# Two passes behind each norm, queries scaled on ScalarE, 32-wide products issued in turn

## Chip, cores and metric

The kernel runs on one core of a Trainium2 chip. The metric is the device time of one execution in microseconds (us); lower is better. Before the change, three executions took 1079.45, 1079.23 and 1076.95 us (median 1079.23).

A core has five engines with instruction streams of their own. TensorE (PE) multiplies matrices; its weight loads are shown apart as PEld. VectorE (DVE) and ScalarE (ACT) do elementwise work, GpSimd (POOL) a little of it, and SyncE (SP) starts most transfers (DMA). Each engine works through its own stream in order and waits at semaphores for the others.

## What is computed

One block of a streaming encoder, on 512 tokens of width 1024, everything in float32: a half-step feed-forward network, a mixer, and a second half-step feed-forward network, each behind an RMS norm that is modulated by a condition vector `c`.

```python
def _modulate(x, shift, scale):
    return _rms(x) * (1.0 + scale[:, None, :]) + shift[:, None, :]
...
        h = _modulate(x, sh1, s1)
        x = x + 0.5 * g1[:, None, :] * _swiglu(h, ffn1_w_in[l], ffn1_w_out[l])
        h = _modulate(x, sh2, s2)
        y = _hybrid_mixer(h, cos, sin, w_in[l], gdn_conv_w[l], gdn_a_log[l], gdn_dt_bias[l],
...
        x = x + g2[:, None, :] * y
        h = _modulate(x, sh3, s3)
        x = x + 0.5 * g3[:, None, :] * _swiglu(h, ffn2_w_in[l], ffn2_w_out[l])
```

The mixer has two groups of four heads. One is a gated delta rule over chunks of 64 tokens, which needs, per chunk and head, the inverse of a unit lower triangular 64 x 64 matrix (`triangular_solve(M, rhs)` in the reference). The other is attention with low-rank queries and keys, whose queries and keys are RMS-normalised per head and carry a rotary part:

```python
    q_nope, q_rope = qf[..., :MLA_NOPE], qf[..., MLA_NOPE:]
...
    q_nope = _rms(q_nope, qkn_q_nope) * scale
    q_rope = _rope(_rms(q_rope, qkn_q_rope), cos[:, :, None], sin[:, :, None]) * scale
```

## The kernel before

Activations are held transposed: eight k-tiles of 128 channels by 512 tokens (`xT`, and the normalised `h`). A float32 product is made from three matmuls on rounded parts (`mm3`, L266 to L268): high weight by high activation, high weight by low activation, low weight by high activation. So each k-tile of `h` is a pair `hh`, `hl`, and each unit of weights (128 output columns by 1024) a pair `wh`, `wl`. `wr` is the raw weight that SP's queue has loaded; ACT casts it to `wh` (L193), and DVE subtracts for `wl` (L198). For a few units behind a norm (`dma=True`) ACT writes −`wr` into `wl` (L195) and a transfer on POOL's queue adds the rest (L196); this is the `wl<-wr` of the profile. PE writes results to the accumulators `pa` and `pb`.

**Stages**, by the time of the profiled execution: the condition vector's modulation and the first feed-forward network (to about 403 us), latents behind norm 2 (403 to 423), the dense units of the projections, with the delta rule's chain and attention beside them as generators that are advanced a step at a time (445 to 660), the recurrence and the output projection (660 to 715), norm 3 and the second feed-forward network (715 to 1076).

**Behind a norm** stands `first_units` (L489): `n` = 3 units at once, first for the first half of the tokens (256), then for the second. In the first half `lead` units go k-tile by k-tile, as `h` becomes ready, and the others follow whole. `nb` is the generator of the second half's norm (`norm_half`): its steps, taken at the places that `marks` lists, issue the column sum (`colsum`, L513, on PE), its scaling (`ve`, L519, on DVE), the spreading of the result (L441, on PE) and the modulation of the second half. Norm 2 uses `lead` 1 and marks (6, 15, 14), norm 3 `lead` 2 and marks (7, 18, 15). `modulate` makes `h`: DVE writes `hm` or `tm` (L459), ACT `hh` (L461), DVE `hl` (L453), the last one step behind. `matmuls_in_order` fixes PE's order in this part as the code is written. Elsewhere the tile scheduler orders each engine's instructions, so that an edit can move instructions far from it.

**`prep_q`** (from L1739) normalises the queries: squares on ACT, the reciprocal roots on DVE, then for the rotary part `qrx` (L1206) and `rope` (L1830 to L1834, into `qro`) on DVE, four transposes of `qro` on PE (L1768), and for the other part eight multiplications of `upo`, two heads each, on POOL (also L1206, the common helper `mul`). `head_tiles` then transposes `upo` on PE (L1725) and scales it on ACT into `nT`.

**`inverse`** builds the inverse by blocks, for four groups `p` of two chunks each: blocks of 16 and 32 by 128-wide products (L1553, L1559), then for `j` = 0 and 64 and four heads the products `T` by `at` (L1569) and `U` by `Y` (L1577), 32 x 32 each on a tile of PE's array given by `tile_position`, then 64-wide ones (L1587 to L1598). Between the groups' steps other work is interleaved by the scheduler: wide matmuls of the dense units and of `out_attended`, and the attention's `on`, transposed at L1900 once DVE has scaled it. In the dense units of the gate, ACT copies `pa` into `z` (L1921); the next unit needs the accumulator that this frees. ACT's table load stands ahead of the exponentials of the attention (`pr`, L168), whose bias `mx` DVE reduces (L1856).

Of the kernel before, what the change touches and what calls it, by code (L numbers as in the profile page):

```python
# [79 lines left out]
class Block:  # L80
# [408 lines left out]
    def first_units(self, n, nb, lead, marks):  # L489


        units = [self.next_unit(ahead=0) for _ in range(n)]
        ps = [self.acc() for _ in range(n)]
        first = [(kt, i) for kt in range(KT) for i in range(lead)] + [(kt, i) for i in range(lead, n) for kt in range(KT)]
        with self.matmuls_in_order(self.last_mm):
            for half in range(2):
                ts = slice(half * HALF, half * HALF + HALF)
                for at, (kt, i) in enumerate([(kt, i) for kt in range(KT) for i in range(n)] if half else first):
                    self.dense(ps[i], units[i], self.h, ts, kt, kt + 1)
                    if half == 0 and at in marks:  # L500
                        next(nb, None)
                if half == 0:
                    drain(nb)
                    self.prefetch(1)
        return ps
# [1027 lines left out]
    def inverse(self, p):  # L1533
# [32 lines left out]
        for j in (0, 64):  # L1566
            a, b = slice(j, j + 32), slice(j + 32, j + 64)
            for h in range(4):
                nc.tensor.matmul(py[b, 32 * h:32 * h + 32], at[a, h * P + j + 32:h * P + j + 64],  # L1569
                                 t[a, h * P + j:h * P + j + 32], start=True, stop=True, tile_position=(j, j + 32))  # L1570
            nc.scalar.copy(y[b, :P], py[b, :P])
        yield
        pz = self.aux()
        for j in (0, 64):
            a, b = slice(j, j + 32), slice(j + 32, j + 64)
            for h in range(4):
                nc.tensor.matmul(pz[a, 32 * h:32 * h + 32], y[b, 32 * h:32 * h + 32],  # L1577
                                 un[b, h * P + j + 32:h * P + j + 64], start=True, stop=True, tile_position=(j + 32, j))
            nc.vector.tensor_scalar(out=h4(un[a, :])[:, :, j + 32:j + 64],
# [150 lines left out]
    def prep_q(self, q):  # L1730
# [375 lines left out]
```

## Time and profile before

| | before |
|---|---|
| median of three executions | 1079.23 us (1076.95 to 1079.45) |
| profiled execution | 1077.71 us |
| its span, first to last instruction | 1076.0 us |
| mean granted TensorE clock | 0.987 of full speed |
| 128.63 MB read from memory, mean | 122 GB/s over the span |
| DMA, queue q1 | 41.1% of 16 engines' span |

The profile is of one execution. Each row of its lists names an engine, the line of the kernel, the operation and its tiles (output, arrow, inputs; buffer numbers are left out), and in a timeline the start in us from the beginning of the span and the length in us. What stands in square brackets is how long the engine stood idle before the row, and what released it. Matmuls overlap, so that their spacing tells more than their length. A matmul on float32 data is recorded as two, so a stretch of eight records is four matmuls of the program. The granted clock of TensorE is a number between 0 and 1 for a stretch of time; at 0.5 a matmul takes twice as long.

### The profile page before, as it was taken

Reading aid. Unit: us, or ns where it says so; the run is one execution under the profiler, and the core shown is the slowest. Engines: PE = TensorE matmul, PEld = TensorE weight load, DVE = VectorE, ACT = ScalarE, POOL = GpSimd, SP = SyncE. Lnnn points to the kernel's source line nnn. Section 1 sums busy time; section 2 is a strip of 40 time slices with the busy share of each in tenths; the row PEclk is TensorE's granted clock in tenths of the full one; section 3 lists DMA queues with packets and bytes.
Section 4 is the critical chain, followed back from the end, with each engine's and each line's share of the span. In section 5 each row is a group of like instructions: output and inputs, shape, how many; then the busy total and the mean of one; then the engine's idle time right before and its main releaser. Section 6 shows DMA issues by size and latency. Waiting matters only on the chain. (4 is left out here: it accounts for less than half of the span.)

```text
span 1076.0 us, 15659 instructions
## 1 busy us (share of the span) xinstructions
PE 1046.7 (97%) x6183; PEld 899.1 (84%) x6183; DVE 689.4 (64%) x1231; ACT 445.3 (41%) x761; POOL 51.3 (5%) x103
## 2 busy tenths in 40 slices
PE   6999999999999999998999899999999999999998
PEld 5788878788887898887778578988899999999997
DVE  4488983433577445558868644769768787777633
ACT  3342222222222245566575363465534444444322
POOL 1000000000000011102000030220000000000000
PEclk8999999999999999999999898999999999999999
DMA  9989963233698349411203001153432333233222
GB/s 274 277 240 310 301 203 99 81 98 93 199 289 263 95 120 240 113 49 40 79 25 92 26 21 39 40 126 91 129 107 79 118 115 98 83 118 99 67 71 79
DMA packets 203687, 136.85 MB, mean 127 GB/s; under 512 B 13777, under 2 KB 186590, under 8 KB 203614
## 3 DMA queue, kind: packets, MB, share of 16 engines
q1 hardware_dynamic: 202318, 131.14, 41.1%
q0 software_dynamic: 1296, 4.72, 2.4%
q8 instruction: 48, 0.79, 0.3%
q14 instruction: 25, 0.20, 0.1%
HBM read 128.63 MB, written 2.49 MB: 122 GB/s over the span
## 5 line engine op out<-in xcount | busy, mean ns | idle before, releaser
L266 PE MATMUL pa<-hh,wh 128*128 128x512 f32 (+1 forms) x597 | 227.0, 380 | 4.3 <-ACT z L1921 4.3
L268 PE MATMUL pa<-hh,wl 128*128 128x512 f32 (+1 forms) x597 | 225.0, 377 | 2.7 <-DMA wl<-wr 2.7
L267 PE MATMUL pa<-hl,wh 128*128 128x512 f32 (+1 forms) x597 | 224.8, 377 | 0.0
L193 ACT CAST wh<-wr 128x1024 fp32r<-128x1024 f32 (+1 forms) x106 | 108.0, 1019 | 258.3 <-PE pa L267 184.4
L198 DVE TENSOR_TENSOR wl<-wr,wh 128x1024 fp32r<-128x1024 f32 (+1 forms) x97 | 114.4, 1180 | 99.0 <-ACT wh L193 94.5
L266 PE MATMUL pa<-ah,wh 128*128 128x512 f32 (+1 forms) x396 | 145.5, 367 | 0.6 <-DVE xT L873 0.4
L267 PE MATMUL pa<-al,wh 128*128 128x512 f32 (+1 forms) x396 | 144.5, 365 | 0.0
L268 PE MATMUL pa<-ah,wl 128*128 128x512 f32 (+1 forms) x396 | 143.5, 362 | 0.0
L266 PEld LDWEIGHTS pa<-hh,wh 128*128 128x128 f32 x597 | 113.6, 190 | 27.2 <-ACT z L1921 4.7
L268 PEld LDWEIGHTS pa<-hh,wl 128*128 128x128 f32 x597 | 113.5, 190 | 23.1 <-DMA wl<-wr 3.3
L267 PEld LDWEIGHTS pa<-hl,wh 128*128 128x128 f32 x597 | 113.5, 190 | 19.2 <-DVE hl L453 0.4
L268 PEld LDWEIGHTS pa<-ah,wl 128*128 128x128 f32 x396 | 74.8, 189 | 12.0
L266 PEld LDWEIGHTS pa<-ah,wh 128*128 128x128 f32 x396 | 75.2, 190 | 10.4 <-ACT wh L193 1.7
L267 PEld LDWEIGHTS pa<-al,wh 128*128 128x128 f32 x396 | 75.2, 190 | 7.2
L551 DVE SCALAR_TENSOR_TENSOR aa<-ar,sc,aa 128x512 f32<-128x512 f32 x98 | 73.2, 751 | 9.7 <-DMA ar<-in_w_ada 8.5
L846 PE MATMUL pb<-fh,wh 128*128 128x256 f32 x144 | 40.7, 282 | 0.0
L848 PE MATMUL pb<-fh,wl 128*128 128x256 f32 x144 | 40.7, 283 | 0.0
L848 PE MATMUL pb<-hh,wl 128*128 128x256 f32 x144 | 40.7, 283 | 0.0
L847 PE MATMUL pb<-fl,wh 128*128 128x256 f32 x144 | 40.7, 282 | 0.0
L847 PE MATMUL pb<-hl,wh 128*128 128x256 f32 x144 | 40.7, 282 | 0.0
L846 PE MATMUL pb<-hh,wh 128*128 128x256 f32 x144 | 40.6, 282 | 0.0
L873 DVE SCALAR_TENSOR_TENSOR xT<-pa,mod,xT 128x512 f32<-128x512 f32 (+1 forms) x40 | 29.4, 736 | 17.5 <-PE pa L268 17.5
(433 smaller groups left out, 1995.0 us busy)
## 6 DMA issues: line engine op xcount, KB each, us to landing
wr<-in_ffn_w_in SPq DMA_DIRECT2D x82, 512.0 KB, 4.1
ar<-in_w_ada SPq DMA_DIRECT2D x48, 512.0 KB, 5.9
wr<-in_ffn_w_out SPq DMA_DIRECT2D x34, 512.0 KB, 3.4
ar<-in_w_ada SPq DMA_DIRECT2D x48, 256.0 KB, 4.8
wr<-in_w_in SPq DMA_DIRECT2D x21, 512.0 KB, 3.9
wr<-in_ffn_w_out SPq DMA_DIRECT2D x17, 384.0 KB, 3.4
wl<-wr POOLq DMA_DIRECT2D x9, 512.0 KB, 5.6
wr<-in_w_out SPq DMA_DIRECT2D x8, 512.0 KB, 4.8
```

The source lines that it names most:

```text
L193: self.nc.scalar.copy(hi, raw)
L198: self.nc.vector.tensor_tensor(out=lo, in0=raw, in1=hi.bitcast(F32), op=ALU.subtract)
L266: mm(out, wh, xh, start=start, stop=False)
L267: mm(out, wh, xl, start=False, stop=False)
L268: mm(out, wl, xh, start=False, stop=stop)
L551: nc.vector.scalar_tensor_tensor(out=acc, in0=a, scalar=sc, in1=acc, op0=ALU.mult, op1=ALU.add)
L846: mm(out, wh, xh, start=start and k == 0, stop=False, **kw)
L847: mm(out, wh, xl, start=False, stop=False, **kw)
L848: mm(out, wl, xh, start=False, stop=stop and k == 3, **kw)
L873: nc.vector.scalar_tensor_tensor(out=self.xT[t][:, ts], in0=p[:, ts], scalar=gate[:, t:t + 1], in1=self.xT[t][:, ts], op0=ALU.mult, op1=AL ...
```

## The change

Three edits, in `first_units`, `inverse` and `prep_q`.

```diff
@@ first_units
-                for at, (kt, i) in enumerate([(kt, i) for kt in range(KT) for i in range(n)] if half else first):
-                    self.dense(ps[i], units[i], self.h, ts, kt, kt + 1)
-                    if half == 0 and at in marks:
+                if half:
+                    for kt in range(KT):
+                        for i in range(n):
+                            self.dense(ps[i], units[i], self.h, ts, kt, kt + 1)
+                    continue
+                parts = [(kt, i, 0, x) for kt, i in first for x in range(2)]
+                parts += [(kt, i, 1, 0) for i in range(n) for kt in range(KT)]
+                for at, (kt, i, y, x) in enumerate(parts):
+                    nc.tensor.matmul(ps[i][:, ts], units[i][y][:, kt, :], self.h[kt][x][:, ts],
+                                     start=kt + x + y == 0, stop=y == 1 and kt == KT - 1)
+                    if at % 3 == 2 and at // 3 in marks:
                         next(nb, None)
-                if half == 0:
-                    drain(nb)
-                    self.prefetch(1)
+                drain(nb)
+                self.prefetch(1)
@@ inverse (and the same for pz, U and Y)
-        for j in (0, 64):
-            a, b = slice(j, j + 32), slice(j + 32, j + 64)
-            for h in range(4):
+        for h in range(4):
+            for j in (0, 64):
+                a, b = slice(j, j + 32), slice(j + 32, j + 64)
                 nc.tensor.matmul(py[b, 32 * h:32 * h + 32], at[a, h * P + j + 32:h * P + j + 64],
                                  t[a, h * P + j:h * P + j + 32], start=True, stop=True, tile_position=(j, j + 32))
+        for j in (0, 64):
+            b = slice(j + 32, j + 64)
             nc.scalar.copy(y[b, :P], py[b, :P])
@@ prep_q
-                qv = q[b][g][:, :384].rearrange("p (h d) -> p h d", h=2)[:, :, :128]
-                self.mul(qv, qv, self.bc(rqn[:, 4 * b + 2 * g:4 * b + 2 * g + 2], 2), nc.gpsimd)
+                for e in range(2):
+                    qv, c = q[b][g][:, 192 * e:192 * e + P], 4 * b + 2 * g + e
+                    nc.scalar.activation(qv, qv, AF.Copy, scale=rqn[:, c:c + 1])
```

In the first half of the tokens, `first_units` issues all products with the high weights first (`hh` and `hl` of each k-tile), unit by unit as before, and all products with the low weights behind them. The same matmuls are issued in another order, and the norm's steps are counted by every third matmul. In `inverse`, the products for `j` = 0 and `j` = 64 alternate, and the two copies of their results follow both. In `prep_q`, sixteen activations on ACT, one for each head and block of tokens, do what eight multiplications on POOL did.

**PE in norm 3.** The program's PE stream at the start of norm 3; `pa_6522` and `pa_6523` are the accumulators of the two leading units (`pa_6530` and `pa_6531` after the change), with weights `wh`, `wl` of their own. Before:

```order
3044 L266 MATMUL pa_6522<-hh_6301,wh_6368 128x256
3045 L267 MATMUL pa_6522<-hl_6302,wh_6368 128x256
3046 L268 MATMUL pa_6522<-hh_6301,wl_6369 128x256
3047 L266 MATMUL pa_6523<-hh_6301,wh_6419 128x256
3048 L267 MATMUL pa_6523<-hl_6302,wh_6419 128x256
3049 L268 MATMUL pa_6523<-hh_6301,wl_6420 128x256
3050 L266 MATMUL pa_6522<-hh_6303,wh_6368 128x256
```

After:

```order
3034 L507 MATMUL pa_6530<-hh_6309,wh_6376 128x256
3035 L507 MATMUL pa_6530<-hl_6310,wh_6376 128x256
3036 L507 MATMUL pa_6531<-hh_6309,wh_6427 128x256
3037 L507 MATMUL pa_6531<-hl_6310,wh_6427 128x256
3038 L507 MATMUL pa_6530<-hh_6311,wh_6376 128x256
...
3082 L507 MATMUL pa_6532<-hl_6324,wh_6474 128x256
3083 L441 MATMUL pb_6591<-dg_6564,ones_97 128x256
3084 L507 MATMUL pa_6530<-hh_6309,wl_6377 128x256
```

Four matmuls of each k-tile of `h` stand where six stood, and the first product with a low weight now stands behind all 48 with high ones and behind the spreading at L441. The column sum keeps its place, behind six k-tiles of the two leading units. On DVE, the `tm` of the last k-tile moves ahead of `ve`.

**ACT in `prep_q`.** ACT's stream where the attention's queries are scaled; `cv` is a convolution's result, `l2q` and `ktk` come from transposed keys of the delta rule, `wh` is the next unit's high weight. Before:

```order
259 L1320 ACTIVATE vn_4041<-pa_4205,ry_3787 128x256
260 L168 ACTIVATE cv_4200<-cv_4200 128x512
261 L1430 ACTIVATE l2q_4269<-pb_4264 128x512
262 L1433 COPY ktk_4271<-pb_4264 128x512
263 L193 CAST wh_4625<-wr_4624 128x1024
```

After:

```order
260 L1789 ACTIVATE upo_3832<-upo_3832,sq_4094 128x128 x2
261 L1789 ACTIVATE upo_3916<-upo_3916,sq_4094 128x128
262 L168 ACTIVATE cv_4200<-cv_4200 128x512
263 L1789 ACTIVATE upo_3916<-upo_3916,sq_4094 128x128
264 L1789 ACTIVATE upo_3850<-upo_3850,sq_4094 128x128 x2
265 L1789 ACTIVATE upo_3934<-upo_3934,sq_4094 128x128 x2
266 L1438 ACTIVATE l2q_4269<-pb_4264 128x512
267 L1441 COPY ktk_4271<-pb_4264 128x512
268 L1789 ACTIVATE upo_3868<-upo_3868,sq_4094 128x128 x2
269 L1789 ACTIVATE upo_3952<-upo_3952,sq_4094 128x128 x2
270 L1789 ACTIVATE upo_3886<-upo_3886,sq_4094 128x128 x2
271 L1789 ACTIVATE upo_3970<-upo_3970,sq_4094 128x128 x2
```

Eight activations stand ahead of `l2q` and eight between `ktk` and the cast of `wh`, which follows next. The eight multiplications leave POOL's stream; nothing takes their place there.

**PE beside the attention.** PE's stream where a dense unit of the gate ends, with the transposes of `on` and the scores `nT` by `nT`. Before:

```order
2601 L266 MATMUL pa_5349<-hh_3169,wh_5227 128x512
2602 L1900 MATMUL pb_5182<-ident_92,on_5180 128x128 x4
2603 L1553 MATMUL pb_5197<-t_5193,at_4551 128x128 x4
2604 L1847 MATMUL pb_5204<-nT_4530,nT_4359 128x256
2605 L1847 MATMUL pb_5205<-nT_4543,nT_4384 128x256
2606 L1850 MATMUL pb_5204<-krT_4426,qrT_4298 128x256
2607 L1850 MATMUL pb_5205<-krT_4426,qrT_4298 128x256
2608 L267 MATMUL pa_5349<-hl_3170,wh_5227 128x512
2609 L268 MATMUL pa_5349<-hh_3169,wl_5228 128x512
```

After:

```order
2601 L266 MATMUL pa_5357<-hh_3169,wh_5235 128x512
2602 L267 MATMUL pa_5357<-hl_3170,wh_5235 128x512
2603 L268 MATMUL pa_5357<-hh_3169,wl_5236 128x512
2604 L1913 MATMUL pb_5190<-ident_92,on_5188 128x128 x4
2605 L1561 MATMUL pb_5205<-t_5201,at_4559 128x128 x4
2606 L1860 MATMUL pb_5212<-nT_4538,nT_4367 128x256
```

The unit's last two matmuls moved ahead of the transposes of `on`. Further on in the same stream stand the small products of the four groups, `U` by `Y`. Before (`pb_5572` is group 0, `pb_5590` 1, `pb_5601` 2, `pb_5622` 3):

```order
2700 L1577 MATMUL pb_5572<-U_5331,Y_5441 32x32 x4
2701 L1577 MATMUL pb_5590<-U_5361,Y_5479 32x32 x4
2702 L1577 MATMUL pb_5601<-U_5397,Y_5513 32x32 x4
2703 L1577 MATMUL pb_5572<-U_5331,Y_5441 32x32 x4
2704 L1577 MATMUL pb_5622<-U_5423,Y_5544 32x32 x2
...
2712 L267 MATMUL pa_5618<-ml_5563,wh_5466 128x512
2713 L1577 MATMUL pb_5601<-U_5397,Y_5513 32x32 x4
2714 L1587 MATMUL pb_5650<-ident_92,U_5397 64x64
2715 L1577 MATMUL pb_5622<-U_5423,Y_5544 32x32 x4
```

After:

```order
2696 L1587 MATMUL pb_5580<-U_5339,Y_5449 32x32 x8
2697 L1587 MATMUL pb_5598<-U_5369,Y_5487 32x32 x8
2698 L1587 MATMUL pb_5609<-U_5405,Y_5521 32x32 x8
2699 L1587 MATMUL pb_5630<-U_5431,Y_5552 32x32 x8
2700 L1599 MATMUL pb_5641<-ident_92,U_5339 64x64 x4
2701 L266 MATMUL pa_5626<-mh_5570,wh_5474 128x512
```

Each group's eight products now stand together, `j` = 0 and 64 in turn, and the four groups one behind the other; before, three stretches held them. For `T` by `at`, seven stretches become three in the same way. The transposes of `U` (L1587 before, L1599 after), three pieces before, are four after, with wide matmuls between them.

More of the change, by code (lines that the diff above doesn't have):

```diff
@@ L489, in first_units @@
     def first_units(self, n, nb, lead, marks):
+        nc = self.nc
         units = [self.next_unit(ahead=0) for _ in range(n)]
@@ L1573, in inverse @@
         pz = self.aux()
-        for j in (0, 64):
-            a, b = slice(j, j + 32), slice(j + 32, j + 64)
-            for h in range(4):
+        for h in range(4):
+            for j in (0, 64):
+                a, b = slice(j, j + 32), slice(j + 32, j + 64)
                 nc.tensor.matmul(pz[a, 32 * h:32 * h + 32], y[b, 32 * h:32 * h + 32],
                                  un[b, h * P + j + 32:h * P + j + 64], start=True, stop=True, tile_position=(j + 32, j))
+        for j in (0, 64):
+            a = slice(j, j + 32)
             nc.vector.tensor_scalar(out=h4(un[a, :])[:, :, j + 32:j + 64],
```

## The prediction

> **What bounds the kernel now.** I read first the busy table of the page, then PE's waits over the whole span (columns: total us, times, longest us), then windows around the stages that the change touches (columns: busy us of PE, PEld, DVE, ACT and POOL, then the granted clock, DMA share and GB/s).
>
> ```profile
> PE 1046.7 (97%) x6183; PEld 899.1 (84%) x6183; DVE 689.4 (64%) x1231; ACT 445.3 (41%) x761; POOL 51.3 (5%) x103
> ```
> ```profile
> PE pa L266 <- ACT z L1921: 4.3, 1, 4.3
> PE pb L1768 <- DVE qro L1834: 2.8, 2, 2.6
> PE pa L268 <- DMA wl<-wr: 2.7, 2, 2.0
> PE pb L1900 <- DVE on L1206: 1.8, 3, 0.9
> ```
> ```profile
> 598.60:605.50 6.90, 4.89 (x17) 4.22 (x18) 3.89 (x6) 2.55 (x7) 0.00 (x0) 0.51 0.25 76
> 642.00:654.00 12.00, 12.00 (x82) 10.24 (x83) 4.68 (x8) 2.92 (x7) 0.00 (x0) 0.57 0.03 7
> 718.10:721.50 3.40, 3.40 (x16) 3.40 (x17) 2.35 (x6) 1.88 (x5) 0.84 (x1) 0.50 1.09 249
> ```
>
> TensorE is busy for 97% of 1076.0 us. The change removes no matmul, so it can only win idle time of PE (1076.0 − 1046.7 = 29 us, much of it at the start), matmul time spent at half clock (the three windows), and time between small products. Four waits are in its reach, 11.6 us together.
>
> **The queries on ScalarE.** Rows of PE, POOL, DVE and ACT around the start of `prep_q`'s products, then the durations of DVE's operations over the whole run (min/median/max in ns), then ACT's operations on 128x128 (mean ns of one behind the busy time).
>
> ```profile
> 497.02 0.66 PE L1768 MATMUL pb<-ident,qro 128*128 128x128 f32 x4 [2.60 <-DVE qro L1834]
> 490.80 5.62 POOL L1206 TENSOR_TENSOR upo<-upo,sq 128x256 f32<-128x256 f32 x8 [23.95 <-DVE sq L189]
> 491.25 2.17 DVE L1206 TENSOR_TENSOR qrx<-upo,sq 128x128 f32<-128x128 f32 x4
> 493.45 0.99 DVE L1830 TENSOR_TENSOR rt<-qrx,rope 128x512 f32<-128x512 f32 x1
> 494.36 1.58 DVE L1833 TENSOR_TENSOR rt<-qrx,rope 128x256 f32<-128x256 f32 x2
> L1206 DVE TENSOR_TENSOR qrx<-upo,sq x8: 277/295/699, 491.2 to 498.1; 128x128 f32<-128x128 f32 x8
> L1833 DVE TENSOR_TENSOR rt<-qrx,rope x4: 417/623/829, 494.4 to 499.3; 128x256 f32<-128x256 f32 x4
> L1830 DVE TENSOR_TENSOR rt<-qrx,rope x2: 691/840/989, 493.5 to 498.4; 128x512 f32<-128x512 f32 x2
> 499.28 1.05 ACT L193 CAST wh<-wr 128x1024 fp32r<-128x1024 f32 x1 [5.59 <-PE pa L267]
> L1879 ACT COPY ao<-pb 128x128 f32<-128x128 f32 x16 | 4.1, 266 | 6.3 <-PE pb L1877 6.1
> L1660 ACT ACTIVATE o<-pb,eG 128x128 f32<-128x128 f32 x12 | 3.4, 370 | 4.7 <-PE pb L1658 4.7
> ```
>
> PE waits 2.60 us for `qro`, which DVE makes while POOL multiplies (490.80 to 496.42). Each kind of DVE operation has its longest duration there and its shortest after POOL is done: 0.70 against 0.28 us, 0.83 against 0.42, 0.99 against 0.69. Without POOL's eight rows the four `qrx` take about 4 × 0.28 instead of 2.17 (−1.05), L1830 −0.30, the two L1833 −0.74 and L1834, of L1830's shape, −0.30: together −2.4, and up to −2.6 with the gaps between them. `qro` is then there at 494.4 to 494.6, and PE arrives at 497.02 − 2.60 = 494.42. ACT takes 16 activations for this, 16 × 0.27 to 16 × 0.37 = 4.3 to 5.9 us by the two rows. The order puts eight ahead of `l2q` and eight between `ktk` and the `wh` cast, into a gap of 5.59 us in which ACT waits for PE to free `wh`. With PE 2.6 earlier that gap is some 3 us, but half of the activations run ahead of it, in ACT's earlier idle time. At 0.27 us ACT is done at about 496.6, when the cast may start (499.28 − 2.6); at 0.37 the cast is 1.5 late. Bounds: −2.6 and 0 (nothing won if as much is waited for ACT); I take **−2.5**, because the wait's own row shows what DVE loses.
>
> **The stall before `z`.** The order moves, by the scheduler, the last two matmuls of a dense unit (L267, L268) ahead of the transposes of `on`, of the inverse's 128-wide products and of the scores.
>
> ```profile
> 595.59 0.50 PE L267 MATMUL pa<-hl,wh 128*128 128x512 f32 x1
> 600.61 0.80 PE L266 MATMUL pa<-hh,wh 128*128 128x512 f32 x1 [4.29 <-ACT z L1921]
> 596.12 1.05 ACT L193 CAST wh<-wr 128x1024 fp32r<-128x1024 f32 x1 [6.80 <-PE pa L267]
> 597.19 1.28 ACT L168 ACT_TABLE_LOAD   x1
> 595.88 0.42 DVE L1856 TENSOR_REDUCE mx<-pb 128x1 f32<-128x256 f32 x1
> ```
>
> Before, the cast waits for that L267, and the table load, the exponentials and the copy `z` queue behind it on ACT. Moved up, L267 is done some 3 us sooner, and the cast with it. The table load then waits for `mx` only, 595.88 + 0.42 = 596.30 instead of 597.19: **−0.9**. Bounds: 0 (if something else holds the cast) and −2.6, if the first 1.7 us of the half clock behind the stall go too; I keep the half clock, since 3.4 us of waiting remain.
>
> **The products of 32 in the block inverse.** PE's rows at one stretch, and at the long one.
>
> ```profile
> 633.17 0.39 PE L267 MATMUL pa<-ml,wh 128*128 128x512 f32 x1
> 633.40 0.40 PE L268 MATMUL pa<-mh,wl 128*128 128x512 f32 x1
> 633.73 0.43 PE L1569 MATMUL pb<-T,at 32*32 32x32 f32 x8
> 634.09 0.50 PE L267 MATMUL pa<-ml,wh 128*128 128x512 f32 x1
> 634.43 0.39 PE L268 MATMUL pa<-mh,wl 128*128 128x512 f32 x1
> 637.13 1.52 PE L1577 MATMUL pb<-U,Y 32*32 32x32 f32 x48
> ```
>
> The 48 records at 637.13 take 1.52 us, some 30 ns each, so the 64 of each kind take 1.9 us. One stretch of 8 costs more than its products: from 633.40 to 634.43 stand two wide matmuls (0.23 each, as from 633.17 to 633.40) and 8 × 0.03, 0.70 in all; 1.03 pass, so a stretch costs 0.33 beside its products. In the order the stretches of `T,at` go from seven to three and those of `U,Y` from three to one, while the 64-wide transposes of `U` stand in one piece more. Taken alone that is 1.3 less for `T,at`, but PE waits there for `on` (1.8 us in three waits, the last row of that table above), and what comes earlier mostly lengthens those: I count −0.3 (bounds 0 and −1.3). For `U,Y` and after it, nothing waits like that: 0.33 × (2 − 1) = −0.3, and what neighbours on different tiles save by overlapping, which no row isolates; it lies between 0 and half of 1.9, and I take −0.7. The clock is 0.57 over the 12 us behind this (642 to 654), about 12 × 0.43 = 5 us lost; moving the small products may take or add one window of 3.4 us (1.7 us either way), which I count at 0. Sum **−1.3**, bounds +1.7 and −4. [...]
>
> **First token half, norm 3 (FFN2).** PE's and DVE's rows.
>
> ```profile
> 718.01 0.51 PE L268 MATMUL pa<-hh,wl 128*128 128x256 f32 x1 [1.96 <-DMA wl<-wr]
> 725.21 0.59 PE L441 MATMUL pb<-dg,ones 128*128 128x256 f32 x2
> 719.36 0.88 DVE L453 SCALAR_TENSOR_TENSOR hl<-tm,mod,hh 128x256 fp32r<-128x256 f32 x2
> 722.42 0.16 DVE L519 TENSOR_SCALAR ve<-pb 128x2 f32<-128x2 f32 x1 [1.80 <-PE pb L513]
> 723.56 0.49 DVE L453 SCALAR_TENSOR_TENSOR hl<-tm,mod,hh 128x256 fp32r<-128x256 f32 x1 [0.18 <-ACT hh L461]
> ```
>
> The wait of 1.96 us for a low weight goes, and with it a window at half clock: by the third window above its 16 matmuls take 3.40/16 = 0.21 us at clock 0.50, so some 0.12 at full clock (the half and a little), and 1.5 us are lost. That looks like −3.5. But the high pass uses a k-tile's four matmuls in 0.48 us, where the six of before took 0.72, and `h` isn't ready so early: `hl` of k-tiles 4 and 5 ends at 720.24. So PE now waits for DVE: k-tile 5 ends at 720.24 + 0.5, colsum at 721.1. `ve` (now behind `tm` of k-tile 7) follows at 721.3 instead of 722.42, `hl` of k-tile 7 ends near 722.3 instead of 724.05, and k-tile 7 is through at 722.8. With 16 high matmuls of the third unit (1.92) L441 starts at 724.7 against 725.21, and 24 matmuls follow in both: −0.5. If these waits leave a window at half clock, about 24 matmuls cost 0.09 more: +1.6. I take **0**, between them and nearer the first; the full −3.5 is the lower end of this term.
>
> **Norm 2 (latents).** Here no low weight is waited for, PE waits for `na` alone, and the next row is the last `hl`.
>
> ```profile
> 407.21 0.58 PE L513 MATMUL pb<-ones,na 128*128 128x1 f32 x4 [1.27 <-DVE na L477]
> 406.25 0.48 DVE L453 SCALAR_TENSOR_TENSOR hl<-hm,mod,hh 128x256 fp32r<-128x256 f32 x1 [0.86 <-ACT hh L461]
> ```
>
> The one leading unit now has two matmuls for a k-tile instead of three and meets `hl` of k-tile 7 at 406.73; by the marks five more matmuls (0.6) and then colsum follow, at about 407.5: **+0.3**; with a window at half clock +1.9.
>
> When does a window at half clock follow? Three more windows, each 3.4 us ahead of the time in question:
>
> ```profile
> 714.70:718.10 3.40, 1.44 (x13) 1.23 (x11) 2.69 (x7) 3.40 (x6) 0.85 (x1) 1.00 0.98 165
> 595.20:598.60 3.40, 1.12 (x6) 0.35 (x4) 2.30 (x5) 2.45 (x3) 0.00 (x0) 1.00 0.00 0
> 404.05:407.45 3.40, 2.13 (x17) 1.75 (x15) 1.53 (x4) 2.47 (x5) 1.66 (x3) 1.00 0.99 183
> ```
>
> The first two, with PE busy for 42% and 33%, were followed by half clock; the third, with 63% (norm 2 as it is), was not. What I work out for the changed norms lies between the last two kinds (about 1.9 of 3.4 us at both, 56%), nearer the third, which is why the forecast keeps full clock and the other outcome stays in. [...]
>
> **Sum**: −2.5 − 0.9 − 1.3 + 0 + 0.3 = −4.4 us. The remaining reordering (`kro`, attention from 545 to 563) I count at nothing, because the wide matmuls there are the same and only fill other waits. Against the profiled execution (1077.7 us: span 1076.0 and 1.7 around it) this gives 1073.3; that execution lies 1.5 below the median of the runs (1079.2), so I put the time between, at **1074.0** (0.7 above the sum, as with the rivals). A measurement of this kernel can tell about 0.3% (3.2 us) from no change.
>
> **Rivals.**
> - The first half is bound by `h`, not weights, and both norms get a window at half clock: +1.9 and +1.6 instead of +0.3 and 0, so −1.2 in all, 1077.2. For it: the 42% window. Chance 0.25, with the case in which ACT's activations give back half of the 2.5.
> - Everything goes: norm 3 wins its 3.5, and the inverse is rid of a half-clock window: −4.4 − 3.5 − 1.7 = −9.6, 1068.8. Against it: DVE's rows of `hl`. Chance 0.1.
> - The small products don't overlap and the removed stretches end in the wait for `on`: −4.4 + 1.3 = −3.1, 1075.3; the change doesn't do there what it says. Chance 0.1.
> - Slower: ScalarE becomes the bound in `prep_q`. If one activation with a scale from memory takes d, the cast is 16 × d − 4.4 us late; above d = 0.43 (2.5 us late) this part's gain is gone, above 0.55 the whole sum, and at 0.75 it is 7.6 late: +3.2, 1081.6. Against it: the 0.27 and 0.37 rows. Chance 0.08.
> - Forecast: 0.47.
>
> The forecast's own spread (about ±2) puts a quarter of its chance (0.12) within 0.3%, with all of the first rival and half of the third: faster 0.35 + 0.1 + 0.05 = 0.50, within 0.42, slower 0.08. The range goes from the second rival to beyond the first, 1068.5 to 1079.0, and leaves out the slower case and the edges.
>
> **What would show it.** Right: no POOL rows in `prep_q`, 16 activations of about 0.3 us, and the wait for `qro` under 0.3; the wait for `z` near 3.4; in norm 3 no wait for `wl<-wr` but three or four short ones for `hl`, with L441 at most 0.5 earlier than now; `U,Y` in one stretch of about 1.2 us. Wrong: clock 0.5 around either norm, the `wh` cast behind the activations as PE's releaser, or a wait for `on` that grows by more than the stretches give.

## The result and the profile after

The changed kernel takes **1074.13 us** (median of 21 executions, 1071.31 to 1079.33) against 1078.64 us of the kernel before (21 executions): ratio **0.9959**, 95% interval 0.9947 to 0.997, so 3 to 6 us or 0.4% faster. The profiled execution took 1074.32 us, span 1072.6, mean granted clock 0.989.

First PE's waits in the changed kernel, as before (total us, times, longest):

```profile
PE pa L266 <- ACT z L1934: 4.1, 1, 4.1
PE pb L1913 <- DVE on L1214: 3.2, 3, 1.6
PE pa L507 <- ACT hh L461: 1.6, 3, 0.8
PE pa L268 <- DMA wl<-wr: 0.9, 1, 0.9
PE pa L507 <- DVE hl L453: 0.7, 2, 0.5
```

The wait for `qro` (2.6 us) is gone and that for `wl` at norm 3 too (the 0.9 is a later one, 0.72 before). In their place stand 2.3 us for `hh` and `hl` at the norms, and the wait for `on` grew from 1.8 to 3.2. The waits of the four rows that I had in reach add up to 8.2 us instead of 11.6, plus those 2.3 new ones.

Windows of the changed kernel (busy us of PE, PEld, DVE, ACT, POOL; then the clock):

```profile
404.20:407.60 3.40, 2.40 (x13) 1.60 (x13) 1.40 (x4) 2.34 (x5) 1.68 (x3) 1.00 1.07 221
407.60:411.00 3.40, 3.40 (x18) 3.40 (x17) 0.64 (x3) 0.00 (x0) 0.82 (x2) 0.50 1.10 225
598.70:605.60 6.90, 6.00 (x22) 5.21 (x23) 4.06 (x6) 1.43 (x3) 0.00 (x0) 0.51 0.00 0
642.00:654.00 12.00, 12.00 (x108) 10.46 (x107) 6.39 (x11) 3.81 (x7) 0.00 (x0) 1.00 0.15 45
714.80:721.60 6.80, 6.58 (x32) 6.28 (x31) 2.01 (x7) 0.91 (x2) 0.88 (x1) 0.50 1.02 237
```

In this pair of profiles half clock is new at norm 2 (407.6 to 411.0), twice as long at norm 3 (6.8 us against 3.4), the same behind `z`, and gone behind the inverse: 642 to 654 had clock 0.57 before and has 1.00 now. It is one execution of each kernel; the profiles of the experiments show further down which of this belongs to the change.

**Where the time went.** The same instruction's start in both profiled executions, and how the lead changes:

| PE's instruction | before | after | lead | change on the way |
|---|---|---|---|---|
| first matmul behind norm 2 | 403.00 | 403.05 | +0.05 | |
| L441 behind norm 2 | 410.60 | 412.46 | +1.86 | +1.8, another +0.2 at a later `wl` |
| first transpose of `qro` | 497.02 | 496.34 | −0.68 | −2.7 |
| first matmul behind the wait for `z` | 600.61 | 599.60 | −1.01 | −0.3 |
| first of `U,Y`, 32 wide | 637.13 | 636.29 | −0.84 | +0.2 |
| first matmul behind norm 3 | 715.29 | 709.67 | −5.62 | −4.8 |
| L441 behind norm 3 | 725.21 | 721.86 | −3.35 | +2.3 |

From there to the end nothing changes (the spans differ by 3.4). So in this pair the norms cost 4.3, the queries won 2.7, and the stretch behind the first `U,Y` won 4.8, nearly all of it by the clock: 10.2 us at half clock are 5.1 lost.

**A measure for the clock.** Every execution reports its span and its mean granted clock. While PE is busy, time at half clock is about half lost: there 512-wide matmuls follow one another every 0.427 us against 0.227 at full clock, and 128-wide ones on float32 data every 0.213 against 0.109 (both profiles). So (1 − clock) × span is about what half clock cost that execution, and the time less this is what it would take at full clock. For the 21 executions of the changed kernel the first is 11.3 us in the mean and the second 1063.0 with a standard deviation of 0.6, while the times themselves spread over 8 us. The spread is the clock's. Both numbers stand with each experiment below; before has 13.5 to 15.7 and 1063.8 to 1064.4 in its 83 executions beside them. By these means the change is worth about 1 us at full clock (0.8 to 1.4), and the larger part of its gain is half clock (2.2 to 4.4).

### The profile page after: what moved, and what is told of

It reads as the page before. It is cut to its first block, busy times and chain, and to the rows that moved or that the text cites. A ratio compares the mean times of both kernels' runs of the same rounds, so it can differ in the third digit from the quotient of the medians.

```text
span 1072.6 us, 15669 instructions
## 1 busy us (share of the span) xinstructions
PE 1044.5 (97%) x6183; PEld 897.1 (84%) x6183; DVE 687.2 (64%) x1231; ACT 448.2 (42%) x777; POOL 45.6 (4%) x95
## 4 chain that ended last, share of the span: by engine, by line
PE 86%; DVE 5%; ACT 5%; DMA 2%; issue 1%; POOL 1%; SPq 0%; POOLq 0%; DVEq 0%; ACTq 0%
PE pa L266 19%; PE pa L267 19%; PE pa L268 19%; PE pb L854 5%; PE pb L855 5%; PE pb L856 5%; PE pa L507 2%; PE pb L1860 1%; PE pb L414 1%; PE pb L266 1%; PE pb L267 1%; PE pb L268 1%; PE pb L1476 1%; PE pb L1863 1%; DVE wl L198 1%
## 5 line engine op out<-in xcount | busy, mean ns | idle before, releaser
L266 PE MATMUL pa<-hh,wh 128*128 128x512 f32 (+1 forms) x549 | 212.6, 387 | 4.1 <-ACT z L1934 4.1
L268 PE MATMUL pa<-hh,wl 128*128 128x512 f32 (+1 forms) x549 | 210.2, 383 | 0.9 <-DMA wl<-wr 0.9
L267 PE MATMUL pa<-hl,wh 128*128 128x512 f32 (+1 forms) x549 | 210.3, 383 | 0.0
L267 PE MATMUL pa<-al,wh 128*128 128x512 f32 (+1 forms) x396 | 144.5, 365 | 0.0
L266 PEld LDWEIGHTS pa<-hh,wh 128*128 128x128 f32 x549 | 103.6, 189 | 27.0 <-ACT z L1934 4.5
L268 PEld LDWEIGHTS pa<-hh,wl 128*128 128x128 f32 x549 | 103.6, 189 | 21.2 <-DMA wl<-wr 1.4
L267 PEld LDWEIGHTS pa<-hl,wh 128*128 128x128 f32 x549 | 103.7, 189 | 18.6 <-issue 0.3
L267 PEld LDWEIGHTS pa<-al,wh 128*128 128x128 f32 x396 | 75.2, 190 | 7.2
L559 DVE SCALAR_TENSOR_TENSOR aa<-ar,sc,aa 128x512 f32<-128x512 f32 x98 | 73.1, 750 | 12.5 <-DMA ar<-in_w_ada 11.3
```

What stands on the lines that cost most here:

```text
L266: mm(out, wh, xh, start=start, stop=False)
L267: mm(out, wh, xl, start=False, stop=False)
L268: mm(out, wl, xh, start=False, stop=stop)
L559: nc.vector.scalar_tensor_tensor(out=acc, in0=a, scalar=sc, in1=acc, op0=ALU.mult, op1=ALU.add)
```

## Experiments

The kernel before ran beside them each time, on the same chip. In all tables "lost" is (1 − clock) × span and "rest" the time less that, means in us.

### The three parts apart

`x1_queries` has the hunk of `prep_q` alone, `x2_inverse` the two of `inverse`, `x3_first` that of `first_units`; `x4_no_first` is the changed kernel without the last:

```diff
 x4_no_first, in the changed kernel
-                parts = [(kt, i, 0, x) for kt, i in first for x in range(2)]
-                parts += [(kt, i, 1, 0) for i in range(n) for kt in range(KT)]
...
+                for at, (kt, i) in enumerate([(kt, i) for kt in range(KT) for i in range(n)] if half else first):
+                    self.dense(ps[i], units[i], self.h, ts, kt, kt + 1)
```

> The kernel before with the queries scaled on ScalarE, and nothing else. Theory P (each part brings what the two profiles show at its place): the wait for qro of 2.6 us goes, L1833 back to 0.4 us; the rest up to the gate's stall is about even, so -2.5 us against before (ratio 0.9977). Rival K (the gain is given back where kro is waited for, since DVE's subtraction for wl moves ahead of the rope of the keys): -1.0 us or less (0.999 to 1.0). Rival A (ScalarE becomes the bound): the cast of wh is PE's releaser there, and the time is not below before.

> The kernel before with the products of 32 issued in turn, and nothing else. Theory P: 64 records of U,Y in 1.2 us, T,at in three stretches, and no half clock between 640 and 655 us, so -4 to -5 us (ratio about 0.996). Rival W (the half clock of 10.2 us behind the inverse went by chance of where the stage lies in the clock's raster, not by the edit): half clock there again, of 6.8 to 10.2 us, and -1.2 us or less (0.999). Rival O (the saving ends in the wait for on): that wait grows by as much as the products save and the time stays within 0.5 us.

> The kernel before with the first token half in two passes, and nothing else. Theory P (the high pass runs ahead of h, PE idles behind ACT and DVE and the clock falls to half at both norms): +4 us (ratio 1.0037), one window of 3.4 us at half clock at norm 2 and one or two at norm 3. Rival W (where the windows fall is chance, they cost as much in before): -0.2 us, within 0.1%, and half clock at norm 2 in no more than the one case. My forecast had +0.3 us for the two norms together.

> The changed kernel with the order of before in the first token half, the other two parts kept. Theory P: norm 2 without half clock, norm 3 with the wait for wl of 2.0 us and one window at half clock as in before, so -4 us against the changed kernel and -8 us against before (ratio 0.9925). Rival W: within 1 us of the changed kernel (0.996). By the forecast's sum it would be -4.7 us (0.9956).

| kernel | ratio to before (95%) | executions | lost | rest |
|---|---|---|---|---|
| before, beside these | 1 | 25 | 15.1 | 1063.8 |
| x1_queries | 0.9956 (0.9932 to 0.9981) | 12 | 11.4 | 1062.5 |
| x2_inverse | 0.9936 (0.9913 to 0.9958) | 8 | 7.1 | 1064.4 |
| x3_first | 1.0016 (0.9995 to 1.0037) | 12 | 14.8 | 1065.7 |
| x4_no_first | 0.9905 (0.9873 to 0.9937) | 6 | 6.9 | 1062.5 |

Queries and inverse win, clear of noise. For the two passes alone the interval contains 1, so that no loss is shown by the time; it shows in the rest. Together the sizes come to 1.0016 × 0.9956 × 0.9936 = 0.9908, below the 0.9959 of all three, so the ratios of the parts don't simply add up. The 0.9905 of x4 fits theory P, but the same kernel run again gave 0.9952 (x14 below). The rest shows what each does by itself at full clock: queries −1.3 us, inverse +0.6, first half +1.9. The inverse wins nothing there; PE's waits for `on` are 3.6 us in its profile (1.8 before) and take up what the products save. What it wins is half clock, 7.1 lost instead of 15.1. Rival K isn't borne out: PE waits 0.8 us for `kro` in x1 and 0.7 before. But a wait of 0.8 us for `t` is new there, and at full clock x1 wins 1.3 us and not the 2.5 of theory P.

### Is it the work on GpSimd?

`x7_pool_spare` is x1 with the eight multiplications back on GpSimd, with a constant as input and a tile as output that nothing reads:

```diff
+        spare = self.slot(s="spare")
+        sv = spare[:, :256].rearrange("p (h d) -> p h d", h=2)
+                self.mul(sv, self.ident.unsqueeze(1).to_broadcast([P, 2, P]),
+                         self.bc(rqn[:, 4 * b + 2 * g:4 * b + 2 * g + 2], 2), nc.gpsimd)
```

> The queries' part alone (scaled on ScalarE), with the eight multiplications put back on GpSimd, but on a constant into a spare tile that nothing reads. Theory C (the work on GpSimd slows VectorE beside it): L1833 back at 0.8 us, the wait for qro back at 2.6 us, ratio about 1.0. Rival (it was that DVE or PE had to wait for the products on POOL): DVE's rows short, the wait for qro under 0.3 us, ratio as in the queries' part alone, 0.9956.

Ratio 0.9999 (0.998 to 1.0018), rest 1063.9 against 1062.5 of x1. DVE's and PE's rows in the changed kernel, then in x7:

```profile
493.27 0.89 DVE L1214 TENSOR_TENSOR qrx<-upo,sq 128x128 f32<-128x128 f32 x4
494.81 0.75 DVE L1846 TENSOR_TENSOR rt<-qrx,rope 128x256 f32<-128x256 f32 x2
496.34 0.65 PE L1780 MATMUL pb<-ident,qro 128*128 128x128 f32 x4
496.59 2.46 ACT L1789 ACTIVATE upo<-upo,sq 128x128 f32<-128x128 f32 x8
498.95 1.04 ACT L193 CAST wh<-wr 128x1024 fp32r<-128x1024 f32 x1
```
```profile
492.43 6.50 POOL L1206 TENSOR_TENSOR spare<-ident,sq 128x256 f32<-128x256 f32 x8 [23.93 <-DVE sq L189]
495.16 1.59 DVE L1840 TENSOR_TENSOR rt<-qrx,rope 128x256 f32<-128x256 f32 x2
497.82 0.66 PE L1768 MATMUL pb<-ident,qro 128*128 128x128 f32 x4 [1.71 <-DVE qro L1841]
```

Theory C holds. Nothing reads what GpSimd makes here, yet DVE's pair takes 1.59 us beside it instead of 0.75, and PE waits for `qro` again. The wait is 1.71 us and not 2.6, since `qrx` is slowed less here: four take 1.33 us, against 2.17 before and 0.89 in the changed kernel. ScalarE needs 2.46 us for eight activations, 0.31 each, and DVE isn't slowed: the pair of 0.75 us runs beside five of them (494.19 to 495.75).

### Taking turns, or standing together?

`x6_grouped` is x2 with the products of a group together, but not in turn:

```diff
-        for h in range(4):
-            for j in (0, 64):
+        for j in (0, 64):
+            for h in range(4):
```

> The kernel before, with the eight products of 32 of a group issued together (one stretch, the copies behind both), but all of one tile of the array first and then all of the other. Theory D (it is the taking in turn that shortens the stretch and keeps the array active): U,Y again near 30 ns a record, 1.9 us for 64 records instead of 1.2, half clock about as often as in before, ratio 0.998 to 1.0. Theory M (the merged stretches alone do it): as the inverse's part alone, ratio about 0.9936, mean clock 0.993.

Ratio 0.9982 (0.9957 to 1.0006), lost 11.6, rest 1064.0, twelve executions of 1069.1 to 1080.4 us. PE's row for `U,Y` in x6, then in x2:

```profile
636.50 1.51 PE L1579 MATMUL pb<-U,Y 32*32 32x32 f32 x64
```
```profile
634.96 0.63 PE L1904 MATMUL pb<-ident,on 128*128 128x128 f32 x4 [1.64 <-DVE on L1206]
635.51 1.20 PE L1579 MATMUL pb<-U,Y 32*32 32x32 f32 x64
```

64 records in 1.51 us are 24 ns each, in turn 19 ns, and before the change 48 took 1.52, 32 ns each (the length of the last record, 0.2 us, is in all three). Standing together gives some of it and taking turns the rest; of the stretch both theories had a share. The time is theory D's: 0.9982, with half clock from 638.6 to 655.7 in x6's profile. In x2's trace the single records start 5 to 7 and mostly 24 to 26 ns apart by turns, in before mostly 31 or 32. That fits two tiles of the array side by side, each with a record every 32 ns.

### The two norms, and a third unit behind

`x9_norm3_only` keeps the order of before at norm 2. `x8_trailing` does too, and at norm 3 adds the third unit's high products two k-tiles behind the others':

```diff
-        first = [(kt, i) for kt in range(KT) for i in range(lead)] + [(kt, i) for i in range(lead, n) for kt in range(KT)]
+        first = [(kt - lag[i], i) for kt in range(KT + max(lag)) for i in range(n) if 0 <= kt - lag[i] < KT]
...
-            ps = self.first_units(3, nb, 2, (7, 18, 15))
+            ps = self.first_passes(3, nb, (0, 0, 2), (9, 18, 15))
```

> Inverse and queries as in the changed kernel, norm 2 as in before, and at norm 3 two passes in which the third unit trails the other two by two k-tiles, so that each k-tile of h brings six high matmuls instead of four, with the colsum behind 30 matmuls. Theory H (two passes lose because PE outruns h, idles and falls to half clock): no wait for wl, waits for h of under 2 us in all at norm 3, no half clock there, and 1.4 to 3 us below the kernel without passes: ratio 0.988 to 0.989. Rival (h is the bound in any order and the clock falls anyway): as with the low weights in place, 0.990 to 0.993.

> The changed kernel with the order of before at norm 2 alone (norm 3 in two passes as changed). Theory: the passes cost about 2 us at each norm, so this lies halfway between the changed kernel (0.9959) and the one without passes (0.9905), 0.993. If norm 2 alone bears the cost: 0.9905; if norm 3 alone: 0.9959. My forecast had +0.3 and 0.

x8: 0.9953 (0.9923 to 0.9984), lost 11.1, rest 1061.9. x9: 0.9985 (0.9958 to 1.0012), lost 13.6, rest 1062.6. x8's time misses theory H's 0.988 to 0.989, and x9's lies above all three values expected of it. As measurements of the norms both are inconclusive: the times of x8 fall into two heaps, 1065.8 to 1070.6 and 1077.7 to 1078.6, with clocks of 0.992 to 0.998 and of 0.984, six of each. Its profile tells more at the place itself. PE's rows in the changed kernel, then in x8:

```profile
713.37 0.38 PE L507 MATMUL pa<-hh,wh 128*128 128x256 f32 x1 [0.82 <-ACT hh L461]
714.25 0.39 PE L507 MATMUL pa<-hl,wh 128*128 128x256 f32 x1 [0.50 <-DVE hl L453]
716.95 0.58 PE L507 MATMUL pa<-hl,wh 128*128 128x256 f32 x1 [0.22 <-DVE hl L453]
721.86 0.59 PE L441 MATMUL pb<-dg,ones 128*128 128x256 f32 x2
```
```profile
708.12 0.28 PE L525 MATMUL pa<-hh,wh 128*128 128x256 f32 x1
711.82 0.38 PE L525 MATMUL pa<-hh,wh 128*128 128x256 f32 x1 [0.58 <-ACT hh L461]
712.70 0.38 PE L525 MATMUL pa<-hl,wh 128*128 128x256 f32 x1 [0.50 <-DVE hl L453]
716.91 0.59 PE L441 MATMUL pb<-dg,ones 128*128 128x256 f32 x2
```

From the first matmul behind norm 3 to L441 it takes 716.91 − 708.12 = 8.8 us in x8, 9.9 before and 721.86 − 709.67 = 12.2 in the changed kernel. With six matmuls for each k-tile instead of four, PE still waits for `h`, but no half clock follows, in x8's profile as in that of x10 below, which has the same order here.

These three times were not all taken at the same clock, though. The same distance at both norms, in all profiles, in us ("one window" is 3.4 us at half clock):

| order | clock | norm 2 | norm 3 |
|---|---|---|---|
| of before | full | 7.6 (before, x4, x9, x10, x13) | 8.3 (x2, x13), 8.9 (x11) |
| of before | one window | 9.1 (x1, x2, x6, x7, x8, x11, x14) | 9.8 to 10.0 (before, x1, x4, x6, x7, x14) |
| two passes | full | 7.9 (x3) | |
| two passes | one window | 9.4 (changed) | 10.8 (x3), 11.0 (x9) |
| two passes | two windows | | 12.2 (changed) |
| third unit behind | full | | 8.8 (x8, x10) |

Norm 2 in x1, which has the order of before there, then in x3, which has two passes; the two windows are x1's:

```profile
402.12 0.28 PE L266 MATMUL pa<-hh,wh 128*128 128x256 f32 x1
411.20 0.60 PE L441 MATMUL pb<-dg,ones 128*128 128x256 f32 x2
403.40:406.80 3.40, 2.13 (x17) 1.77 (x15) 1.30 (x3) 2.23 (x5) 1.66 (x3) 1.00 0.99 211
406.80:410.20 3.40, 3.40 (x17) 3.40 (x18) 0.64 (x3) 0.00 (x0) 0.72 (x2) 0.50 1.15 234
```
```profile
400.75 0.28 PE L507 MATMUL pa<-hh,wh 128*128 128x256 f32 x1
408.65 0.59 PE L441 MATMUL pb<-dg,ones 128*128 128x256 f32 x2
```

So half clock at norm 2 isn't brought by the two passes: seven of the twelve profiles in the order of before have it, and of two with two passes one. At the same clock two passes cost 0.3 us there. At norm 3 they cost 0.9 to 1.1 at the same clock, and all three profiles with them have half clock, against six of nine in the order of before. The third unit behind avoids it in both of its profiles, but at full clock it takes 0.5 us longer than the order of before, with its wait for `wl`, does in x2 (the last row is a window behind this wait):

```profile
708.86 0.28 PE L266 MATMUL pa<-hh,wh 128*128 128x256 f32 x1
711.48 0.39 PE L268 MATMUL pa<-hh,wl 128*128 128x256 f32 x1 [1.85 <-DMA wl<-wr]
717.18 0.59 PE L441 MATMUL pb<-dg,ones 128*128 128x256 f32 x2
712.20:715.60 3.40, 3.40 (x31) 3.40 (x30) 3.00 (x10) 1.85 (x4) 1.31 (x2) 1.00 1.06 243
```

This wait of 1.85 us isn't followed by half clock, while the 1.96 of before is. Theory H's cause, PE running ahead of `h`, is thus supported for norm 3 by five profiles and not needed for norm 2.

### What sets the half clock?

In the profiles of before and the changed kernel every change of the clock lies a whole number of steps of 3.413 us behind the first one: 1, 3, 172, 174, 185, 188, 207 and 208 steps in before, 1, 3, 116, 117, 172, 174, 206 and 208 in the changed kernel, all to within 0.01 us. From one execution to another this raster stands elsewhere: the half clock behind `z` ends at 604.1 us in x2 and at 605.3 in x13, the same kernel. For each window of the raster, in the 14 profiles, I added up, from PE's rows, the time that each matmul's columns take at full clock (0.23 us for 512, as they follow one another; twice that for float32 data taken in two records, whose 128 columns follow every 0.109 us) times the share of the array's 128 rows that it uses. In the profiles of before and the changed kernel, from 100 us on, 555 windows stand at full clock: the six that come to 38% of the window or less were followed by half clock, and none of the others, from 40% up, was. In the 14 profiles there are some 3800. All 39 of those that come to at most 39% were followed by half clock; of those from 40% up one was, at 43%. Of the windows at half clock, all 38 that come to at most 40% were followed by another, and all 40 above it by full clock (in before and the changed kernel five at 19 to 37% and six at 42 to 54%). At half clock, with 512 columns every 0.427 us instead of 0.227, some 53% fits into a window, so that 40% is three quarters of what can stand there. These are counts of what followed in these profiles; why the clock falls, no run shows.

The small products use a quarter or half of the rows, so that PE can be busy without a gap and the sum still be small: from 639.6 to 643.0 in before PE is busy for all 3.40 us, and the window comes to 36%. By this sum over x8's trace, half of all positions of the raster have a window of at most 39% between the wait for `on` and the end of `U,Y`, and where half clock came there, it lasted 10.2 us (before) to 20.5 (x10). At norm 2 it is 42% of the positions in the order of before (x13's trace) and 44% with two passes (x3's); at norm 3 44% in the order of before (x2's), at least 80% with two passes (x9's) and 3% with the third unit behind (x8's).

Theory W was made from the first eight runs' profiles (its 0.37 is the 39% of these counts with a slightly shorter time for a column); these four tried it, by adding 20 wide matmuls to the inverse (`x10_filled` on x8, `x11_before_filled` on before), and by running two kernels again:

```diff
+        hh = self.h[0][0]
+        fill = lambda p: nc.tensor.matmul(p[:, 256:], hh[:, :P], hh[:, :256], start=True, stop=True)
...
         py, y = self.aux(), self.slot(s="Y")
+        fill(py)
```

> The kernel with trailing third unit, with 20 added matmuls of 128 x 256 whose results nothing reads, one at each of the last five steps of each of the four groups' inverse. Theory W (half clock follows any window of 3.41 us in which the rows of PE's array are used for less than about 0.37 of the time; the inverse falls under it in about half of all positions of the raster and then stays at half clock for 10 to 17 us): 20 x 0.12 = 2.4 us dearer at full clock, but no half clock between 625 and 655 us in any execution, so that the two heaps of times (near 1067 and 1078 us) become one near 1071, with a mean clock of 0.992 to 0.994. Rival (the half clock there has another cause): the two heaps stay, both 2.4 us higher, 1069 and 1080.

> The kernel before with the same 20 added matmuls, nothing else. Theory W: 2.4 us dearer at full clock, no half clock between 625 and 655 us, and so 1 to 3 us faster than before in the mean though it computes more: ratio 0.997 to 0.999. Rival: 2.4 us slower, ratio 1.002, half clock there as often as in before.

> The inverse's part alone once more, the same kernel. Its 8 executions all missed the half clock behind the inverse, while by its trace half of all positions of the raster would meet it. Theory W: that was the raster's position, which is alike in executions that follow one another; now some executions meet it, the time at full clock is again 1064 to 1065 us (as before's), and the ratio comes nearer to 1, 0.996 to 1.0. Rival D (the products in turn keep the clock up): again 0.9936 and a mean clock of 0.993 in every execution.

> The changed kernel with the order of before in the first token half, once more, the same kernel (6 executions so far). Theory W: time at full clock again near 1062.5 us, half clock lost in some executions as in the kernel with the trailing unit, ratio 0.994 to 0.997, so even with the changed kernel within 2 us. Rival P (the first token half's part costs 4 to 6 us): again 0.9905.

| kernel | ratio to before (95%) | executions | lost | rest |
|---|---|---|---|---|
| before, beside these | 1 | 23 | 15.7 | 1063.9 |
| x10_filled | 1.0025 (1.001 to 1.004) | 12 | 16.5 | 1065.8 |
| x11_before_filled | 1.0076 (1.0059 to 1.0093) | 5 | 18.0 | 1070.1 |
| x13_inverse_again | 0.9923 (0.9906 to 0.9941) | 6 | 7.1 | 1064.5 |
| x14_no_first_again | 0.9952 (0.9928 to 0.9976) | 12 | 12.4 | 1061.7 |

The filling failed, and its rival wasn't right either: x10's two heaps are gone, but into the upper one (clocks of 0.980 to 0.987), and x11 is 0.8% slower than before, 6.2 us of it at full clock, with half clock from 643.3 to 663.7 in its profile. PE's rows in x10 show why.

```profile
633.53 0.63 PE L1939 MATMUL pb<-ident,on 128*128 128x128 f32 x4 [1.31 <-DVE on L1232]
633.92 0.36 PE L1567 MATMUL pb<-hh 128*128 128x256 f32 x1
634.21 0.44 PE L1610 MATMUL pb<-U,Y 32*32 32x32 f32 x16
634.58 0.38 PE L1567 MATMUL pb<-hh 128*128 128x256 f32 x1
634.89 0.44 PE L1610 MATMUL pb<-U,Y 32*32 32x32 f32 x16
```

Each added matmul splits the stretch of small ones. From one to the next it takes 634.58 − 633.92 = 0.66 us, where its own columns take 0.11 and sixteen small ones 0.25 (at the mean spacing of 16 ns in x2): 0.30 for the split. The prediction's price of a separate stretch (0.33) should have been in my expectation. The window from 633.9 comes to 36% by the sum above, and half clock follows from 637.4 to 657.8. That agrees with the counts and doesn't prove that this sum decides: no run here raised the share and kept the clock.

x14 comes out as theory W has it: 0.9952, and not again rival P's 0.9905. That is within 2 us of the changed kernel's 0.9959, as theory W said; x4's gap of 6 us to it isn't repeated.

x13 decides against theory W for the inverse alone: with x2 it has now run 14 times, at mean clocks of 0.988 to 0.997, where x8's six slower executions had 0.984. At most the one at 0.988 can have met the half clock behind the inverse. Chance hardly does that if half of the raster's positions are open. In both of its profiles the half clock behind `z` ends at a step of the raster (604.1 and 605.3), and the next steps lie at nearly the same place of the program, although the raster stands elsewhere at the start: 631.4 with `on` at 634.96 in x2, 632.6 with `on` at 635.94 in x13, 3.5 and 3.4 us ahead. Between the half clock behind `z` and the inverse the positions are thus not evenly spread, and in x2 they miss the sparse window; with the queries' part, which brings PE to `z` and to `on` at other times, some don't (x14: 12.4 lost, x4: 6.9, the same kernel). That half clock pulls the raster into step with the program is an inference from two profiles, and no run tested it.

By the sum, the edit doesn't make the sparse positions fewer, it moves them. In the order of before (x1's trace) the window has to start 1.9 to 3.6 us behind the first `U,Y`, 48% of the positions; in turn (x2's) 3.1 to 1.4 us ahead of it, 50%. The kernel before has a step of the raster 2.5 us behind, and the window from there comes to 36%. In x2 and x13 steps lie 2.8 and 2.9 us behind and 4.1 and 3.9 ahead, and the windows come to 45% or more. x4 has a step 1.8 us ahead, its window comes to 32%, and half clock follows. No run moved the raster alone, so this stays worked out from the traces and not tested.

## Why the prediction came out right

The time was forecast at 1074.0 and is 1074.1. That is luck: the sum was right by errors of opposite sign, and most of what the forecast had wrong is half clock, which differs between executions of the same kernel (mean clocks of 0.984 to 0.992 in the 21 of the changed one). Three rows of the changed kernel, for the stall before `z`:

```profile
592.82 1.13 PE L1561 MATMUL pb<-t,at 128*128 128x128 f32 x8 [0.77 <-DVE t L1214]
595.67 0.42 DVE L1869 TENSOR_REDUCE mx<-pb 128x1 f32<-128x256 f32 x1
596.17 1.28 ACT L168 ACT_TABLE_LOAD   x1 [4.34 <-DVE mx L1869]
```

- **Queries**, −2.5 forecast: −2.7 at the place, ScalarE needs 0.31 us for an activation, the cast of `wh` starts at 498.95 behind the last eight, and PE's list of waits has no row for it. x7 shows the cause that was argued. Over the whole kernel the part is worth 1.3 us at full clock and 3.7 less half clock, which the forecast didn't have. A wait of 2.6 us can itself be followed by half clock, as in x3's profile (495.0 to 498.4), but of the six profiles with this wait that is the only one, so where the 3.7 come from stays open.
- **The stall before `z`**, −0.9 forecast: the table load starts at 596.17, released by `mx`, as argued, but the gain is 0.3. The forecast left `mx` where it was; it starts at 595.67 instead of 595.88, and 0.7 had been won ahead of it. PE now waits 0.8 us for `t` before the 128-wide products, and the scores and `mx` stand behind these. The wait for `z` is 4.1 instead of 3.4, since PE too arrives earlier: the two matmuls moved ahead no longer stand behind the scores. The step "moved up, L267 is done some 3 us sooner" was right, what it is worth wasn't.
- **Products of 32**, −1.3 forecast: seven stretches and three became three and one, and `T,at` won next to nothing because of `on`, as forecast. `U,Y` took 1.2 us, as forecast; the −0.7 for neighbours on different tiles was an estimate that no row of before isolates, and here the records start 6 to 7 and 25 ns apart by turns, against 32 before. The term that failed is the half clock behind it, "which I count at 0": it was worth 5.1 us in this pair of profiles, and the bound of −4 was too near. It isn't the edit's in every execution: in the profiles of x4 and x9, which have it, 17.1 us at half clock stand there, and x1 without it has none. Of the 8 us less half clock in x2 and x13, 5.1 belong to this place by the profiles of before and x13, and 1.7 to norm 3, which the edit doesn't touch.
- **Norm 3**, 0 forecast: +2.3 in this pair, 0.9 to 1.1 at the same clock. The waits for `h` came as worked out (no wait for `wl`, short ones for `hh` and `hl`), but they left two windows at half clock, one more than my upper end of +1.6 had. The step that failed is "nearer the third, which is why the forecast keeps full clock": 56% was the busy share by the view, which counts each matmul's tail (a 256-wide row is 0.28 us long, and the next starts 0.12 behind it); the window 711.4 to 714.8 has 1.94 of 3.40 busy by the same view, 57%, and by columns only 30%. x1's window at norm 2 shows that the busy share can't decide it: 2.13 of 3.40 busy, 63% as in the forecast's third window, and half clock follows.
- **Norm 2**, +0.3 forecast: +1.8 in this pair, the case priced at +1.9, with half clock from 407.6 to 411.0. But the order of before meets that as often; at the same clock it is the +0.3 of the forecast (7.9 against 7.6 and 9.4 against 9.1).
- The windows at half clock at the norms of the changed kernel came without a long wait of PE: the longest ahead of them are 0.44 us at norm 2 and 0.82 at norm 3.

In the profile of the changed kernel the first rival (half clock at both norms) thus happened, together with a part of the second (no half clock behind the inverse). Two kernels with less of the change came out below it: the inverse's part alone, at 0.9936 and 0.9923 of before in two sessions, and the change without the two passes, at 0.9905 and 0.9952, against 0.9959 of the whole; they were not timed side by side with it.

## What to carry to other kernels

Price a wait on TensorE with what can follow it: here a sparse window of 3.4 us was followed by another at half clock, 1.7 us more, so that a reordering which trades one long wait for several short ones can lose. Before a window at half clock is put down to an edit, look whether kernels without that edit have it too: at norm 2 seven of twelve profiles did. In x10 work put between small products made the sparse stretch longer, by 0.30 us for each split. When times of the same kernel spread by 1%, compare the mean clocks and the times less the clock's share before reading a ratio, and don't add up ratios of parts.

## What the hardware showed that was not expected

- Half clock came behind windows in which little of the array is in use, not behind idle time alone: in x10 PE is busy for all 3.40 us from 633.9, on 32 or 64 rows for the most part, the window comes to 36% by the sum above, and half clock follows. In the profiles of before and the changed kernel the windows of 0 to 38% were followed by it and those from 40% up weren't; at half clock those of 19 to 37% were followed by another, and those of 42 to 54% by full clock.
- Once at half clock amid such products it stayed there for long: 10.2 us before, 17.1 in x4, 20.5 in x10.
- GpSimd's multiplications slowed VectorE's beside them by a factor of two (1.59 us against 0.75 for the pair of the rope in x7), though the rope shares no tile with them.
